# Row sums of a matrix-vector product moved from TensorE and VectorE to GpSimd, in the entry of a transformer trunk

## The chip, the cores and the metric

The kernel runs on one core of a Trainium2 chip. The core has five engines that work side by side, each through its own queue in order: TensorE (PE in the profile: matrix products, results in PSUM), VectorE (DVE), ScalarE (ACT), GpSimd (POOL) and SyncE (SP), which here issues DMAs. They wait for one another through semaphores. The metric is the device time of one execution in microseconds (us); of several runs the median counts.

## The reference

A trunk of two layers on 1024 rows of width 1024, all in float32. Each layer normalizes its input, modulates it by a shift and a scale that come from a conditioning vector `c`, and puts it through a mixer and an MLP. The part at issue is the first layer's modulation and the product behind it:

```python
c_act = jax.nn.silu(c)
mod = c_act @ ada_w[l] + ada_b[l]                  # 1024 x 6144
sh_m, sc_m, g_m, sh_f, sc_f, g_f = jnp.split(mod, 6, axis=-1)
h = modulate(rmsnorm(x, norm_g[l, 0]), sh_m, sc_m) # h * (1 + scale) + shift
bcx = h @ w_in                                     # 1024 x 3072
```

For the mixer's input the kernel needs only `sh_m` and `sc_m`, 2 x 1024 numbers, out of a product with 1024 x 2048 weights (8 MB). They are needed before the first product of the trunk can start.

## The kernel before, in words

The entry (`conv_phase`) makes the first column block of `h @ w_in` while the inputs come in. It works in eight blocks k = 0 to 7 of 128 columns of `h`. The weights of block k's shift and scale lie in a tile `aw[k]`: 128 partitions, 8 rows, 256 columns (128 of the scale, 128 of the shift). There are three such tiles in turn, so block k + 3 is loaded when block k has been read. What is wanted is the sum over 1024 inputs: over the 8 rows (each times its entry of the activated vector, `csil`) and over the 128 partitions. In the end it must stand in PSUM with one column per partition, summed over partitions by TensorE.

The table `rows_on_pe = (4, 4, 4, 4, 0, 0, 0, 0)` says how many of a block's eight rows TensorE takes by itself. For blocks 0 to 3 TensorE multiplies rows 0 to 3 straight from `aw` (`matvec`, 8 products, which the profile shows as 16 instructions), and VectorE sums rows 4 to 7 into a tile `av` (`row_sum`, one instruction a row). For blocks 4 to 7 VectorE sums all eight rows. Then TensorE adds `av` over the partitions with a matrix of ones (`row_end`).

The order of everything in the entry is written out by hand in the string `ENTRY`. Each word is one step, and each engine has its steps in just this order. The steps, with the line of the profile:

- `x`, `a`, `w`: loads of a row tile of x, of half of `aw[k]`, and of the mixer's weights of one block (SyncE, L196). They share one queue.
- `N`, `n`: the norm of a row tile (ScalarE L315 and L317, VectorE L322 and L1125).
- `A`: `matvec` (TensorE, L1018). `Dk.i`: `row_sum`, row i of block k (VectorE, L1025 the first and L1027 the others). `E`: `row_end` (TensorE, L1034). `F`: `shifts`, the scale and shift as columns (VectorE, L1039 and L1041).
- `T`: four transposes of x (TensorE, L1046). `U`, `W`: the modulated operand, rounded and plain (ScalarE, L1059). `L`: their difference (VectorE, L1064).
- `X`, `Y`: the mixer's weights split into two parts (ScalarE L1077, VectorE L1080).
- `M`: nine products of block k with one half of the rows (TensorE, L227). `Z`: products with zeros (TensorE, L1000).

Block k goes through a, A, D, E, F, then U, W, L, then M. A step that waits holds up everything behind it on its engine. GpSimd has no step in `ENTRY`; it fills four constants and `zeros` at the start and an accumulator in each of four later phases.

Of the kernel before, what the change touches and what calls it, by code (L numbers as in the profile page):

```python
# [8 lines left out]
F32 = mybir.dt.float32  # L9
# [3 lines left out]
ALU = mybir.AluOpType  # L13
# [4 lines left out]
P = 128  # L18
# [112 lines left out]
def trunk_kernel(ctx: ExitStack, tc: tile.TileContext, x, ada_w, ada_b, norm_g, conv_in_w, conv_out_w, kv_ada_w,  # L131
                 kv_a_w, kv_b_w, q_a_w, q_b_w, attn_o_w, mlp_up_w, mlp_down_w, columns, ada_first, conv_first,
                 consts, out):
    nc = tc.nc
    uid = [0]

    def nm(s):
        uid[0] += 1
        return f"{s}_{uid[0]}"

    def pool(name, side="left", **kw):
        return tc.alloc_tile_pool(name=name, bufs=1, side=side, reuse_waits="tile", **kw)
# [20 lines left out]
    def mm_ps():  # L163
        return ps.tile([P, HALF], F32, tag="mm", name=nm("mm"))

    def tp_ps():
        return ps.tile([P, HALF], F32, tag="tp", name=nm("tp"))
# [27 lines left out]
    def ld(out_, in_):  # L195
        nc.sync.dma_start(out_, in_)  # L196
# [5 lines left out]
    csil = cp.tile([P, KD], F32, name="csil")  # L202
# [767 lines left out]
    def conv_phase():  # L970
# [15 lines left out]
        st = pool("st", "right")  # L986
# [14 lines left out]

        aw, av, pa, tps, rts, raws, w = ({} for _ in range(7))
        acc = {}
        rows_on_pe = (4, 4, 4, 4, 0, 0, 0, 0)

        def load_x(t):
            ld(xt[t], x0[t * P:(t + 1) * P, :])
# [1 line left out]
        def load_ada(k, i):  # L1009
            if i == 0:  # L1010
                aw[k] = st.tile([P, KD, 2 * P], F32, tag="aw", name=nm("aw"), bufs=3)
            ld(aw[k][:, 4 * i:4 * i + 4, :], ada_first[k][:, 4 * i:4 * i + 4, :])

        def matvec(k):
            pa[k] = mm_ps() if k < 4 else tp_ps()
            for i in range(rows_on_pe[k]):
                for j in range(2):
                    nc.tensor.matmul(pa[k][:, j * P:(j + 1) * P], aw[k][:, i, j * P:(j + 1) * P],  # L1018
                                     csil[:, i:i + 1].to_broadcast([P, P]), start=i == j == 0, stop=False,
                                     skip_group_check=True)  # L1020

        def row_sum(k, i):
            if i == rows_on_pe[k]:
                av[k] = st.tile([P, 2 * P], F32, tag="av", name=nm("av"), bufs=2)
                nc.vector.tensor_scalar(av[k], aw[k][:, i, :], csil[:, i:i + 1], None, op0=ALU.mult)  # L1025
            else:
                nc.vector.scalar_tensor_tensor(av[k], aw[k][:, i, :], csil[:, i:i + 1], av[k], op0=ALU.mult, op1=ALU.add)  # L1027
# [96 lines left out]
        def norm_x(t):  # L1124
            nc.vector.tensor_scalar(xt[t], xt[t], rroot(rts[t]), None, op0=ALU.mult)  # L1125

        verbs = dict(Z=fill, x=load_x, a=load_ada, w=load_w, X=high_w, Y=low_w, N=root, n=norm_x, A=matvec, D=row_sum, E=row_end,
                     F=shifts, T=turn, U=lambda k, half: scaled(k, half, True), W=lambda k, half: scaled(k, half, False),
                     L=scaled_low, M=lambda k, half: products(k, half, acc))
# [68 lines left out]
    bg += ada_fm(ad, "s0f", w0, 4 * D, 32, gain(0, 2))  # L1198
    bg += ada_fm(ad, "h0f", w0, 3 * D, 24)
    conv_phase()  # L1200

    def down_phase(slots, sizes, wd, src_fn, g, xsrc, xdst, next_w, key, ys=None, pairs=True):
# [662 lines left out]
```

## Time and profile before

| | us |
|---|---|
| median of 3 runs | 2084.99 |
| lowest and highest run | 2084.24, 2086.21 |
| the profiled execution's time | 2085.6 |
| its span in the profile | 2083.8 |
| TensorE busy in the span | 2061.7 |
| VectorE busy | 1525.3 |
| ScalarE busy | 1058.7 |
| GpSimd busy | 4.6 |

The span runs from the first instruction to the last, and the execution's own time is 1.8 us longer. The matmuls are pipelined and their ends are modelled, so one that overlaps the next shows up as busy too. The entry is the first 68 us or so. In a row of the timeline the first two numbers are the start and the duration; x16 means that sixteen instructions of one kind are put into one row, and the bracket at the end says how long the engine stood idle before it and what it waited for.

### The profile page before, as it was taken

The numbers are of one execution on the slowest core, as the hardware profiler recorded it, in microseconds if no ns is written. First come the engines' busy times: TensorE is split into PE (matmuls) and PEld (weight loads), VectorE is DVE, ScalarE is ACT, GpSimd is POOL, SyncE is SP. The second block draws the span as 40 slices with busy tenths as digits, with TensorE's granted clock in tenths as the row PEclk, the third lists the DMA queues.
The fourth block names the chain that finished last, engine by engine and source line by source line (L and its number), as shares of the span: only waits on it lengthen the run. The fifth ranks groups of instructions, "written<-read, shape, count | busy, mean of one in ns | idle before, by whom it ended". The sixth has DMA issues, their size and how long they took to land.

```text
span 2083.8 us, 25410 instructions
## 1 busy us (share of the span) xinstructions
PE 2061.7 (99%) x9709; PEld 1716.1 (82%) x9709; DVE 1525.3 (73%) x2119; ACT 1058.7 (51%) x1506; POOL 4.6 (0%) x9
## 2 busy tenths in 40 slices
PE   8999999999999999999999999999999999999998
PEld 6888878888888888888888888878888888888887
DVE  7887776977665668876769999767976665559556
ACT  6533264845444533445756566556744454444342
POOL 0000000000000000000000000000000000000000
PEclk9999999999999999999999999999999999999999
DMA  7435464466443976556323232065455544753343
GB/s 284 116 120 151 142 219 136 120 200 210 152 156 119 325 236 229 163 198 199 98 73 87 76 109 88 31 202 162 113 184 173 187 160 178 268 193 111 101 142 142
DMA packets 222450, 330.86 MB, mean 159 GB/s; under 512 B 17268, under 2 KB 121972, under 8 KB 222328
## 3 DMA queue, kind: packets, MB, share of 16 engines
q1 hardware_dynamic: 184744, 248.68, 38.0%
q10 hardware_dynamic: 37584, 80.56, 10.3%
q8 instruction: 76, 1.25, 0.3%
q14 instruction: 46, 0.38, 0.1%
HBM read 248.45 MB, written 80.74 MB: 158 GB/s over the span
## 4 chain that ended last, share of the span: by engine, by line
PE 88%; DVE 7%; DMA 2%; ACT 2%; issue 1%; SPq 0%; DVEq 0%; ACTq 0%
PE one L227 41%; PE mm L227 20%; PE big L227 11%; PE tp L227 7%; PE big L1628 4%; PE tp L1660 1%; PE tp L1345 1%; DMA raw<-in_ada_w_dram 1%; ACT junk L315 1%; DVE y L366 1%; DMA w<-in_conv_first_dram 0%; DMA aw<-in_ada_first_dram 0%; DVE y L370 0%; PE tp L475 0%; DVE raw L345 0%
## 5 line engine op out<-in xcount | busy, mean ns | idle before, releaser
L227 PE MATMUL one<-slot,uphi 128*128 128x512 f32 x1240 | 381.7, 389 | 0.0
L227 PEld LDWEIGHTS one<-slot,uphi 128*128 128x128 f32 x1240 | 232.8, 188 | 48.4 <-issue 0.5
L227 PE MATMUL big<-slot 128*128 128x512 f32 x1152 | 264.1, 390 | 0.7 <-DVE y L1171 0.4
L227 PEld LDWEIGHTS big<-slot 128*128 128x128 f32 x1152 | 215.5, 188 | 45.7 <-ACT y L941 0.8
L227 PE MATMUL one<-slot,uplo 128*128 128x512 f32 x620 | 243.0, 392 | 2.4 <-DVE y L621 1.6
L230 ACT ACTIVATE ring<-w 128x1024 fp32r<-128x1024 f32 x98 | 103.8, 1059 | 260.5 <-PE tp L227 141.9
L227 PE MATMUL one<-ring,ring 128*128 128x512 f32 x1008 | 229.1, 389 | 0.0
L227 PEld LDWEIGHTS one<-ring,ring 128*128 128x128 f32 x1008 | 189.2, 188 | 39.3
L231 DVE TENSOR_TENSOR ring<-w,ring 128x1024 fp32r<-128x1024 f32 x98 | 119.8, 1223 | 116.8 <-ACT ring L230 116.7
L231 DVE TENSOR_TENSOR uplo<-raw,uphi 128x1024 fp32r<-128x1024 f32 x114 | 139.2, 1224 | 78.8 <-ACT uphi L230 78.8
L230 ACT ACTIVATE uphi<-raw 128x1024 fp32r<-128x1024 f32 x114 | 120.6, 1059 | 136.6 <-PE one L227 67.9
L227 PE MATMUL mm<-ring,ring 128*128 128x512 f32 x672 | 162.7, 390 | 1.2 <-DVE ring L231 1.2
L227 PE MATMUL tp<-ring,ring 128*128 128x512 f32 x672 | 161.6, 389 | 0.0
L227 PEld LDWEIGHTS mm<-ring,ring 128*128 128x128 f32 x672 | 125.5, 188 | 28.4 <-DVE ring L231 2.2
L227 PEld LDWEIGHTS tp<-ring,ring 128*128 128x128 f32 x672 | 126.1, 188 | 26.2
L227 PEld LDWEIGHTS one<-slot,uplo 128*128 128x128 f32 x620 | 116.4, 188 | 27.9 <-DVE y L621 2.4
L227 PE MATMUL mm<-slot,uphi 128*128 128x512 f32 x424 | 130.9, 390 | 0.0
L231 DVE TENSOR_TENSOR ring<-raw,ring 128x1024 fp32r<-128x1024 f32 x98 | 119.5, 1219 | 10.8 <-ACT ring L230 10.8
L227 PE MATMUL one<-slot,s 128*128 128x512 f32 x468 | 112.6, 389 | 1.6 <-DVE s L231 1.6
L256 DVE SCALAR_TENSOR_TENSOR acc<-raw,csil,acc 128x1024 f32<-128x1024 f32 x66 | 84.6, 1282 | 36.1 <-DMA raw<-in_ada_w_dram 35.0
L619 ACT ACTIVATE y<-one 128x512 f32<-128x512 f32 x62 | 36.7, 592 | 142.4 <-PE one L227 112.3
L230 ACT ACTIVATE ring<-raw 128x1024 fp32r<-128x1024 f32 x98 | 102.2, 1045 | 4.2 <-DMA raw<-ha 3.8
(291 smaller groups left out, 3509.3 us busy)
## 6 DMA issues: line engine op xcount, KB each, us to landing
ha<-y ACTq DMA_DIRECT2D x196, 256.0 KB, 3.0
raw<-ha SPq DMA_DIRECT2D x98, 512.0 KB, 4.2
raw<-in_ada_w_dram SPq DMA_DIRECT2D x80, 512.0 KB, 4.2
raw<-in_mlp_up_w_dram SPq DMA_DIRECT2D x70, 512.0 KB, 5.1
w<-in_mlp_down_w_dram SPq DMA_DIRECT2D x56, 512.0 KB, 5.1
raw<-hd SPq DMA_DIRECT2D x24, 512.0 KB, 4.5
xs<-raw ACTq DMA_DIRECT2D x24, 512.0 KB, 3.4
raw<-xs SPq DMA_DIRECT2D x24, 512.0 KB, 4.6
```

Of the source, the lines that this page charges most:

```text
L227: nc.tensor.matmul(out_, lhs[a], rhs[b], start=first and i == 0, stop=last and i == 2, skip_group_check=more)
L230: nc.scalar.activation(hi, src, AF.Copy)
L231: nc.vector.tensor_tensor(lo, src, hi.bitcast(F32), op=ALU.subtract)
L256: nc.vector.scalar_tensor_tensor(acc, raw, s, acc, op0=ALU.mult, op1=ALU.add)
L315: nc.scalar.activation(junk, src, AF.Square, accum_out=ss)
L366: nc.vector.tensor_tensor(y, y, p_, op=ALU.add)
L619: nc.scalar.activation(dst, x_, AF.Copy)
L1345: nc.tensor.transpose(p_[:, t * P:(t + 1) * P], ys[hf * 4 + t][:, k * P:(k + 1) * P], ident)
L1628: nc.tensor.matmul(o_, a, m_, start=j == 0, stop=j == 4)
L1660: nc.tensor.transpose(p_[:, c_:c_ + P], pts[h, 4 * hf + i][:, j * P:(j + 1) * P], ident)
```

## The change

`rows_on_pe` becomes (4, 0, 0, 0, 0, 0, 0, 0). In blocks 1 to 7 GpSimd takes rows 0 to 3: it multiplies them by their entries of `csil` in place (128x1024), adds rows 2 and 3 to rows 0 and 1 (128x512) and then row 1 to row 0 (128x256). VectorE takes rows 4 to 7; its first instruction adds GpSimd's row 0. Block 0 stays as it was.

```diff
-        rows_on_pe = (4, 4, 4, 4, 0, 0, 0, 0)
+        rows_on_pe = (4, 0, 0, 0, 0, 0, 0, 0)
+        pooled = 4
...
+        def pool_sum(k):
+            a = aw[k]
+            nc.gpsimd.tensor_tensor(a[:, :pooled, :], a[:, :pooled, :], csil[:, :pooled].unsqueeze(2).to_broadcast([P, pooled, 2 * P]),
+                                    op=ALU.mult)
+            nc.gpsimd.tensor_tensor(a[:, 0:2, :], a[:, 0:2, :], a[:, 2:4, :], op=ALU.add)
+            nc.gpsimd.tensor_tensor(a[:, 0, :], a[:, 0, :], a[:, 1, :], op=ALU.add)
+
         def matvec(k):
+            if not rows_on_pe[k]:
+                return pool_sum(k)
             pa[k] = mm_ps() if k < 4 else tp_ps()
...
         def row_sum(k, i):
-            if i == rows_on_pe[k]:
+            if not rows_on_pe[k] and i < pooled:
+                if i == 0:
+                    pool_sum(k)
+            elif not rows_on_pe[k] and i == pooled:
+                av[k] = st.tile([P, 2 * P], F32, tag="av", name=nm("av"), bufs=2)
+                nc.vector.scalar_tensor_tensor(av[k], aw[k][:, i, :], csil[:, i:i + 1], aw[k][:, 0, :], op0=ALU.mult, op1=ALU.add)
+            elif i == rows_on_pe[k]:
                 av[k] = st.tile([P, 2 * P], F32, tag="av", name=nm("av"), bufs=2)
                 nc.vector.tensor_scalar(av[k], aw[k][:, i, :], csil[:, i:i + 1], None, op0=ALU.mult)
```

`ENTRY` stays as it is: at the words A1, A2, A3 and at D4.0, D5.0, D6.0, D7.0 the three GpSimd instructions are issued, and the words Dk.1 to Dk.3 of blocks 4 to 7 do nothing. Lines behind the edit shift by 16: L1034 becomes L1050, L1046 L1062, L1064 L1080, L1080 L1096.

TensorE's queue from E0 on, before. The numbers behind the names tell the tiles apart; `tp_323` is filled from rows 0 to 511 of x.

```order
L1034 MATMUL mm_252<-ones,av_266 128x128 x2
L1018 MATMUL mm_295<-csil,aw_261 128x128 x8
L1000 LDWEIGHTS zeros
L1000 MATMUL one_187<-zeros 128x512
L1000 LDWEIGHTS zeros
L1000 MATMUL one_187<-zeros 128x512
L1046 MATMUL tp_323<-cs,y_165 128x128
L1046 MATMUL tp_323<-cs,y_166 128x128
L1046 MATMUL tp_323<-cs,y_167 128x128
L1046 MATMUL tp_323<-cs,y_168 128x128
L1034 MATMUL mm_295<-ones,av_308 128x128 x2
L1018 MATMUL mm_335<-csil,aw_304 128x128 x8
```

The same place with the change:

```order
L1050 MATMUL mm_252<-ones,av_266 128x128 x2
L1000 LDWEIGHTS zeros
L1000 MATMUL one_187<-zeros 128x512
L1000 LDWEIGHTS zeros
L1000 MATMUL one_187<-zeros 128x512
L1062 MATMUL tp_317<-cs,y_165 128x128
L1062 MATMUL tp_317<-cs,y_166 128x128
L1062 MATMUL tp_317<-cs,y_167 128x128
L1062 MATMUL tp_317<-cs,y_168 128x128
L1050 MATMUL mm_325<-ones,av_302 128x128 x2
L227 MATMUL one_344<-slot_151,w_194 128x512
L227 MATMUL one_344<-slot_151,w_193 128x512 x2
```

The rows of A1 and A2 (L1018) are gone, and behind E1 stands M0.0 (L227) at once.

VectorE's queue in block 4 (`av_468`) and the beginning of block 5 (`av_497`), before:

```order
L1025 TENSOR_SCALAR av_468<-aw_418,csil 128x256
L1027 SCALAR_TENSOR_TENSOR av_468<-aw_418,csil,av_468 128x256
L1064 TENSOR_TENSOR b_154<-raw_464,b_154 128x512
L1039 SCALAR_TENSOR_TENSOR sh_180<-mm_423,g_173,b_174 128x1
L1041 TENSOR_TENSOR sh_180<-mm_423,cols 128x1
L1027 SCALAR_TENSOR_TENSOR av_468<-aw_418,csil,av_468 128x256
L1025 TENSOR_SCALAR av_497<-aw_450,csil 128x256
L1027 SCALAR_TENSOR_TENSOR av_468<-aw_418,csil,av_468 128x256
L1027 SCALAR_TENSOR_TENSOR av_497<-aw_450,csil,av_497 128x256
L1027 SCALAR_TENSOR_TENSOR av_468<-aw_418,csil,av_468 128x256
L1064 TENSOR_TENSOR b_155<-raw_501,b_155 128x512
```

With the change block 4 is `av_488`:

```order
L1080 TENSOR_TENSOR b_154<-raw_448,b_154 128x512
L1055 SCALAR_TENSOR_TENSOR sh_180<-mm_455,g_173,b_174 128x1
L1057 TENSOR_TENSOR sh_180<-mm_455,cols 128x1
L1038 SCALAR_TENSOR_TENSOR av_488<-aw_408,csil 128x256
L1080 TENSOR_TENSOR b_155<-raw_485,b_155 128x512
L1043 SCALAR_TENSOR_TENSOR av_488<-aw_408,csil,av_488 128x256 x2
L1080 TENSOR_TENSOR slot_151<-q_161,slot_151 128x512
L1043 SCALAR_TENSOR_TENSOR av_488<-aw_408,csil,av_488 128x256
```

Four of block 4's eight row sums are gone, and the first one left (L1038) reads GpSimd's row of `aw` beside its own. The first rows that GpSimd's queue gains, blocks 1 and 2:

```order
L995 MEMSET zeros 128x512
L1017 ISA
L1017 TENSOR_TENSOR aw_261<-aw_261,csil 128x1024
L1019 TENSOR_TENSOR aw_261<-aw_261 128x512
L1020 TENSOR_TENSOR aw_261<-aw_261 128x256
L1017 TENSOR_TENSOR aw_298<-aw_298,csil 128x1024
L1019 TENSOR_TENSOR aw_298<-aw_298 128x512
```

Ahead of the first product stands one instruction that the order gives no operation for (ISA).

## The prediction

> **What bounds the kernel now.** I read the page first, for the share of each engine in the chain that ended last.
>
> ```profile
> span 2083.8 us, 25410 instructions
> ...
> PE 88%; DVE 7%; DMA 2%; ACT 2%; issue 1%; SPq 0%; DVEq 0%; ACTq 0%
> ```
>
> TensorE sets the end, and the change touches only the entry, so the question is how early TensorE gets its entry done. Next the busy times in stretches of 5 us over the entry:
>
> ```profile
> core 0: us, PE busy (x) PEld busy (x) DVE busy (x) ACT busy (x) POOL busy (x), PEclk, DMA share, GB/s
> 15.00:20.00 5.00, 5.00 (x36) 4.45 (x36) 3.37 (x10) 2.75 (x5) 0.00 (x0) 0.80 1.02 411
> 20.00:25.00 5.00, 5.00 (x36) 4.45 (x34) 4.50 (x12) 4.68 (x10) 0.00 (x0) 1.00 1.04 404
> 25.00:30.00 5.00, 5.00 (x37) 4.53 (x35) 4.53 (x13) 4.11 (x10) 0.00 (x0) 1.00 0.91 300
> 30.00:35.00 5.00, 5.00 (x29) 4.30 (x28) 3.81 (x12) 3.01 (x5) 0.00 (x0) 1.00 1.00 346
> 35.00:40.00 5.00, 4.38 (x26) 3.50 (x25) 5.00 (x12) 2.97 (x5) 0.00 (x0) 1.00 0.73 256
> 40.00:45.00 5.00, 5.00 (x26) 4.11 (x25) 4.62 (x13) 2.51 (x5) 0.00 (x0) 1.00 0.58 211
> 45.00:50.00 5.00, 4.79 (x28) 3.79 (x26) 3.83 (x11) 2.74 (x6) 0.00 (x0) 1.00 0.29 82
> 50.00:55.00 5.00, 5.00 (x29) 4.18 (x28) 4.67 (x13) 3.25 (x6) 0.00 (x0) 1.00 0.30 79
> ```
>
> From 15 us on TensorE is all but full (39.17 of 40 us), VectorE nearly so (34.33 of 40), the DMA engines are full up to 25 us and almost to 35, and GpSimd does nothing. Two engines are tight at once, and the change takes work from both. The timeline of TensorE, at the steps A (products of four rows, L1018), E (sum over partitions, L1034), M (L227) and at each later wait:
>
> ```profile
> 12.85 3.10 PE L1018 MATMUL mm<-csil,aw 128*128 128x128 f32 x16 [4.16 <-DMA aw<-in_ada_first_dram]
> ...
> 18.11 1.95 PE L1018 MATMUL mm<-csil,aw 128*128 128x128 f32 x16
> 19.90 0.59 PE L1000 MATMUL one<-zeros 128*128 128x512 bf16 x2
> ...
> 20.76 0.61 PE L1034 MATMUL mm<-ones,av 128*128 128x128 f32 x4
> 21.21 1.95 PE L1018 MATMUL mm<-csil,aw 128*128 128x128 f32 x16
> 22.92 2.32 PE L227 MATMUL one<-slot,w 128*128 128x512 f32 x9
> ...
> 25.51 0.61 PE L1034 MATMUL mm<-ones,av 128*128 128x128 f32 x4
> ...
> 28.05 1.95 PE L1018 MATMUL mm<-csil,aw 128*128 128x128 f32 x16
> 29.84 0.60 PE L1046 MATMUL tp<-cs,y 128*128 128x128 f32 x4
> ...
> 32.36 0.60 PE L1034 MATMUL mm<-ones,av 128*128 128x128 f32 x4
> ...
> 36.78 0.73 PE L227 MATMUL one<-b,w 128*128 128x512 f32 x2 [0.62 <-DVE b L1064]
> ...
> 49.55 0.63 PE L1046 MATMUL tp<-cs,y 128*128 128x128 f32 x4 [0.21 <-DVE sh L1041]
> ```
>
> The first row is A0; then A1, E1, A2, M0.0, E2, A3, T0.1, E3. After E3 TensorE waits only 0.62 and 0.21 us. VectorE in the same stretch (L1039 and L1041 are an F; L1025 and L1027 are row sums D; L1064 is an L):
>
> ```profile
> 18.31 0.22 DVE L1039 SCALAR_TENSOR_TENSOR sh<-mm,g,b 128x1 f32<-128x1 f32 x1 [0.58 <-PE mm L1034]
> 18.45 0.15 DVE L1041 TENSOR_TENSOR sh<-mm,cols 128x1 f32<-128x1 f32 x1
> 18.51 0.34 DVE L1025 TENSOR_SCALAR av<-aw,csil 128x256 f32<-128x256 f32 x1
> 18.89 1.52 DVE L1027 SCALAR_TENSOR_TENSOR av<-aw,csil,av 128x256 f32<-128x256 f32 x3
> 20.33 0.68 DVE L1064 TENSOR_TENSOR slot<-q,slot 128x512 fp32r<-128x512 f32 x1
> ...
> 22.47 0.35 DVE L1025 TENSOR_SCALAR av<-aw,csil 128x256 f32<-128x256 f32 x1
> ...
> 30.80 0.48 DVE L1027 SCALAR_TENSOR_TENSOR av<-aw,csil,av 128x256 f32<-128x256 f32 x1
> ...
> 53.68 1.00 DVE L1027 SCALAR_TENSOR_TENSOR av<-aw,csil,av 128x256 f32<-128x256 f32 x2
> ```
>
> Here D1 begins at 18.51, D2 at 22.47, D3.7 ends at 31.28 and D7.7 at 54.68.
>
> **TensorE's part.** A1, A2 and A3 go. From the start of each to the start of what follows it is 19.90 - 18.11 = 1.79, 22.92 - 21.21 = 1.71 and 29.84 - 28.05 = 1.79: 5.3 us of a full engine. But it does not reach the end. All three lie ahead of E3, E3 needs D3.7, and no VectorE instruction ahead of D3.7 is dropped: blocks 1 to 3 keep their four D each. D3.7 ended at 31.28 and E3 began at 32.36, so E3 can come at most 1.1 us earlier. Behind E3 TensorE's list is the same, with 0.83 us of waits. The gain is at most 1.1 + 0.8 = 1.9 us, however cheap GpSimd is; the other 3.4 us become waits for E1, E2 and E3.
>
> **VectorE's part.** It loses D4.0-D4.3 to D7.0-D7.3, and the first D of blocks 1 to 3 becomes a form with two tensor operands. Its groups in the first 70 us:
>
> ```profile
> L1027 DVE SCALAR_TENSOR_TENSOR av<-aw,csil,av 128x256 f32<-128x256 f32 x40 | 18.7, 482 | 0.5
> L1125 DVE TENSOR_SCALAR y<-y,small 128x1024 f32<-128x1024 f32 x8 | 6.0, 753 | 0.3
> L1064 DVE TENSOR_TENSOR slot<-q,slot 128x512 fp32r<-128x512 f32 x8 | 5.5, 687 | 1.2 <-ACT slot L1059 1.2
> L1025 DVE TENSOR_SCALAR av<-aw,csil 128x256 f32<-128x256 f32 x8 | 2.8, 350 | 1.6 <-DMA aw<-in_ada_first_dram 1.5
> L322 DVE RECIPROCAL small<-small 128x1 f32<-128x1 f32 x8 | 1.3, 161 | 4.5 <-ACT small L317 4.5
> ```
>
> 4 x (0.35 + 3 x 0.48) = 7.2 us go, 3 x (0.48 - 0.35) = 0.4 us come: 6.8 us less. This too pays only where TensorE waits for VectorE, the same 0.83 us.
>
> **GpSimd's part.** Seven blocks, each one product over 128x1024 and two sums over 128x512 and 128x256, each waiting for the one before. The trace has no GpSimd instruction that reads; nearest are its fills and the loads that release the first product:
>
> ```profile
> 0.73 0.52 POOL L995 MEMSET zeros<- 128x512 bf16 x1 [0.29 <-POOLq L1851]
> ...
> L246 POOL MEMSET acc<- 128x1024 f32 x3 | 2.9, 958 | 805.6 <-DVE uplo L704 726.8 <-DVE w L1080 78.8
> ...
> 5.61 1.57 SPq L196 DMA_DIRECT2D aw<-in_ada_first_dram  x2
> ...
> DMA to landing us min/median/max: 4.7/9.2/11.0
> ```
>
> One pass over 1024 elements is 0.96 us, over 512 0.52, so over 256 about 0.26. Lower bound: one pass each, 1.74 us a block. Upper bound: three passes (two operands in, one out), 5.2 us. I take two, since the fill already pays the writing and two operands must be fetched: 3.5 us, and 0.1 for the waits between: 3.6 us a block. The Trainium skill (GPSIMD Engine Reference, Performance versus the Vector engine) gives 4497 ns for a two-input add of 2048 elements; worked out from that, an estimate of 4.0 us a block, which would put the result below at +15 us instead of +12. No run here shows it yet.
>
> The first product needs the first half of block 1, issued at 5.61: at the longest landing time, 16.6 us. GpSimd alone then ends the blocks at 20.2, 23.8 and 27.4. D1.4 waits 20.2 - 18.5 = 1.7 us more than now, D2.4 1.3 us, D3.4 nothing. Queued behind D1.4 on VectorE are D1.5 to D1.7 and L0.0, for which E1 and M0.0 wait on TensorE. The shift of 1.3 to 1.7 us is partly paid out of A3, gone behind E2: about +1 us at E3, and from there to the end.
>
> **Sharing.** What decides is whether GpSimd and VectorE can read SBUF side by side. The trace cannot show it: GpSimd only writes there. Bounds: they do, +1 us; or only one of them runs at a time. I take the second. Its rows: one operand costs VectorE 753 ns for 1024 elements, 0.74 ns an element; two operands cost 687 for 512, 1.34 ns. One-operand instructions use a second path and two-operand ones need it, so nothing is spare for a third reader unless GpSimd has a path of its own. The Trainium skill (SBUF — State Buffer, Who interferes with whom) says that it has none: a VectorE instruction with two SBUF inputs, or in a two-port mode, and a GpSimd instruction that reads exclude each other for the whole instruction; no run here shows it yet, and by it the time is the one forecast here.
>
> The sum, from 16.6 us to the end of D7.7. VectorE's busy time there: about 2.5 of the first stretch (3.37 less D0's end before 16.6), then 4.50 + 4.53 + 3.81 + 5.00 + 4.62 + 3.83 + 4.67: 33.5. Less the 6.8 dropped: 26.7. Less what reads TensorE's results or single columns, seven F at 0.37 and three reciprocals at 0.16, 3.1: 23.6 us that exclude GpSimd. GpSimd: 7 x 3.6 = 25.2. One after the other: 16.6 + 23.6 + 25.2 = 65.4, against 54.7 now: +10.7. That is without a gap; VectorE stood idle 40 - 34.3 = 5.7 us in these stretches for others' results, and I let a quarter of it remain: +12. E7, F7, the last T, U, W, L and M hang on D7.7 in TensorE's and VectorE's queues and slip by the same. SP slips too: w3 waits for Y1 and a4 to a7 stand behind it; with the DMA engines idle from 45 us on (share 0.29) I add nothing. The profiled execution took 2085.6 us for its span of 2083.8, so 2085.6 + 12 = 2097.6; the median of the runs is 0.6 lower: **2097 us**.
>
> **Rivals.** 0.2% is 4.2 us, about what tells a change from none here.
> 1. No sharing: GpSimd reads without hindering VectorE. Then it is ready for D3 and all later blocks, and only D1 and D2 wait: +1 us, 2086 (from 2083 if GpSimd is at its lower bound, to 2089). For it: the block-1 wait is short and VectorE loses 6.8 us. It decides if VectorE's L1064 stays at 687 ns beside a running product.
> 2. GpSimd late or slower than I take it, without sharing: at 5.2 us a block it ends block 7 at 16.6 + 36.4 = 53 and D7.4-D7.7 (1.9 us) at 55, E2 some 4 to 5 us late: +5, 2090. The order shows an unnamed instruction ahead of its first product, without a price in the trace; the queue stands empty from 1.25 to 16.6, so 15 us of it are hidden and each one above comes on top of D1.4's wait. The Trainium skill (GPSIMD Engine Reference, Instruction dispatch) gives about 6 us for the first call of freshly loaded code: an estimate, and hidden here.
> 3. Faster by what TensorE loses, -5.3 us, 2080: needs GpSimd's sums by 18.5 and VectorE ahead of TensorE up to E3; 9.0 busy of 10 us between 20 and 30 speaks against it.
>
> **How the numbers follow.** Sharing 0.63, late or slow 0.14, no sharing 0.20, faster 0.03. In the likeliest case the lower bound of the price gives 16.6 + 23.6 + 7 x 1.9 = 53.5, no later than now but for D1 and D2, so +2; the upper 16.6 + 23.6 + 7 x 5.3 = 77.3: +23 and the gaps. TensorE's clock can add: A0, behind a wait of 4.16 us, took 3.10 us, into the stretch with a granted clock of 0.80, where A1 took 1.95. Ends near both bounds are unlikely together with sharing, so its own range is 2089 to 2107. No sharing lies around 2086, and the range that holds 8 in 10 takes most of it in: 2085.5 to 2107. Slower by over 0.2%: 0.63 x 0.96 + 0.14 x 0.8 + 0.20 x 0.1 + 0 = 0.74, to which I add a few hundredths for what only costs (clock, SP's queue): 0.78. Within: 0.19. Faster: 0.03.
>
> **What would show it.** Right: E1 at 22 to 25 instead of 20.76 with TensorE waiting for VectorE; L1038 rows released by GpSimd; L1064 and the other two-operand rows longer than 687 ns, or idle, beside a running product; E7 near 67 instead of 55.74; the same rows as now behind it. Wrong: two-operand rows at their old length beside GpSimd and E7 within 3 us of 55.74 (rival 1); GpSimd's product beginning after 17 us with its load long landed (rival 2); E3 before 31 (rival 3).

## The result, and the profile after

The changed kernel takes 2098.78 us (median of 6 runs, 2097.14 to 2101.01) against 2084.61 us before (median of 6, 2083.45 to 2086.21): the ratio is 1.0068, 95% interval 1.0055 to 1.0081. That is 14.2 us slower, where +12 was forecast.

The page of the changed kernel: the span, the busy times, and the chain by engine.

```profile
span 2096.0 us, 25328 instructions
...
PE 2063.1 (98%) x9660; PEld 1716.3 (82%) x9661; DVE 1536.1 (73%) x2103; ACT 1059.0 (51%) x1506; POOL 34.0 (2%) x30
...
PE 88%; DVE 7%; ACT 2%; DMA 2%; issue 1%; POOL 0%; SPq 0%; DVEq 0%; ACTq 0%; POOLq 0%
```

VectorE was given less to do and is busy for longer: 1536.1 us against 1525.3. Its groups in the first 80 us of the changed kernel say which rows grew (the last two columns ahead of the bar are the sum in us and the mean in ns):

```profile
L1043 DVE SCALAR_TENSOR_TENSOR av<-aw,csil,av 128x256 f32<-128x256 f32 x24 | 16.9, 702 | 0.5
L1038 DVE SCALAR_TENSOR_TENSOR av<-aw,csil 128x256 f32<-128x256 f32 x7 | 9.3, 1326 | 5.1 <-POOL aw L1020 5.1
L1141 DVE TENSOR_SCALAR y<-y,small 128x1024 f32<-128x1024 f32 x8 | 8.2, 1030 | 0.3
L1080 DVE TENSOR_TENSOR slot<-q,slot 128x512 fp32r<-128x512 f32 x8 | 6.6, 823 | 2.0 <-ACT slot L1075 2.0
```

In the kernel before, instructions of the same four forms had 482, 482, 753 and 687 ns. GpSimd's timeline beside VectorE's shows where the extra comes from. GpSimd, block 1 and the products of blocks 2 and 4:

```profile
16.65 1.89 POOL L1017 TENSOR_TENSOR aw<-aw,csil 128x1024 f32<-128x1024 f32 x1 [15.39 <-DMA aw<-in_ada_first_dram]
18.62 1.59 POOL L1019 TENSOR_TENSOR aw<-aw 128x512 f32<-128x512 f32 x1
20.29 0.72 POOL L1020 TENSOR_TENSOR aw<-aw 128x256 f32<-128x256 f32 x1
20.97 1.89 POOL L1017 TENSOR_TENSOR aw<-aw,csil 128x1024 f32<-128x1024 f32 x1
...
39.60 2.27 POOL L1017 TENSOR_TENSOR aw<-aw,csil 128x1024 f32<-128x1024 f32 x1 [8.38 <-DVE av L1043]
```

And VectorE's timeline of the same kernel:

```profile
16.95 2.14 DVE L1141 TENSOR_SCALAR y<-y,small 128x1024 f32<-128x1024 f32 x1
...
21.05 2.10 DVE L1038 SCALAR_TENSOR_TENSOR av<-aw,csil 128x256 f32<-128x256 f32 x1 [1.76 <-POOL aw L1020]
23.18 2.75 DVE L1043 SCALAR_TENSOR_TENSOR av<-aw,csil,av 128x256 f32<-128x256 f32 x3
25.84 0.68 DVE L1080 TENSOR_TENSOR slot<-q,slot 128x512 fp32r<-128x512 f32 x1
...
44.06 2.10 DVE L1038 SCALAR_TENSOR_TENSOR av<-aw,csil 128x256 f32<-128x256 f32 x1 [3.31 <-POOL aw L1020]
```

GpSimd's second product runs from 20.97 to 22.86. VectorE's D1.4 starts beside it at 21.05 and ends at 23.15: 0.3 us after the product, and 2.10 us instead of 0.48. L0.0 at 25.84, with no GpSimd instruction beside it, has its old length. It works the other way too: GpSimd's sum at 18.62 takes 1.59 us, while the shortest of its kind takes 1.28.

What TensorE waits for in the first 90 us of the changed kernel (us in total, how many times, the longest), with the rows of E1, M0.0, E2, E4 and E7 in its timeline:

```profile
PE mm L1050 <- DVE av L1043: 6.6, 2, 4.4
...
PE one L227 <- DVE b L1080: 4.3, 1, 4.3
PE tp L1062 <- ACT slot L1075: 2.3, 1, 2.3
...
PE tp L1050 <- ACT b L1075: 0.9, 1, 0.9
```

```profile
25.98 1.22 PE L1050 MATMUL mm<-ones,av 128*128 128x128 f32 x4 [4.44 <-DVE av L1043]
26.86 3.66 PE L227 MATMUL one<-slot,w 128*128 128x512 f32 x9
...
33.07 1.14 PE L1050 MATMUL mm<-ones,av 128*128 128x128 f32 x4 [2.12 <-DVE av L1043]
...
53.43 1.20 PE L1050 MATMUL tp<-ones,av 128*128 128x128 f32 x4 [0.91 <-ACT b L1075]
...
71.20 0.61 PE L1050 MATMUL tp<-ones,av 128*128 128x128 f32 x4
```

E1 is 5.2 us late (25.98 against 20.76), E2 7.6, E4 14.3 (53.43 against 39.16) and E7 15.5 (71.20 against 55.74). The loss is made in blocks 1 to 4, and behind E4 TensorE runs through. The new waits are 6.6 + 4.3 + 2.3 + 0.9 = 14.1 us. The old ones of 0.8 and TensorE's dropped 5.3 come off: 8.0. The other 7.5 us of the 15.5 stand in slower products: M0.0 takes 3.66 instead of 2.32, and the granted clock is 0.52 between 25 and 30 us, where the kernel before had 1.00. Whether those 7.5 us are a cause of their own is asked below.

The profiled executions lie 12.2 us apart at the end, not 15.5. About 2.6 us of this is seen in later waits: the kernel before had waits of 0.8 and 1.2 us that the changed one doesn't have, and one of 1.6 us that is now 1.0. In the kernel before:

```profile
PE one L227 <- DVE s L231: 1.6, 1, 1.6
...
PE mm L227 <- DVE ring L231: 1.2, 1, 1.2
...
PE one L227 <- ACT y L689: 0.8, 1, 0.8
```

These belong to one execution each; over all runs the difference is 14.2.

### The profile page after: what moved, and what is told of

It is laid out like the page before. It is cut to its first block, busy times and chain, and to the rows that moved or that the text cites. A ratio compares the mean times of both kernels' runs of the same rounds, so it can differ in the third digit from the quotient of the medians.

```text
span 2096.0 us, 25328 instructions
## 1 busy us (share of the span) xinstructions
PE 2063.1 (98%) x9660; PEld 1716.3 (82%) x9661; DVE 1536.1 (73%) x2103; ACT 1059.0 (51%) x1506; POOL 34.0 (2%) x30
## 4 chain that ended last, share of the span: by engine, by line
PE 88%; DVE 7%; ACT 2%; DMA 2%; issue 1%; POOL 0%; SPq 0%; DVEq 0%; ACTq 0%; POOLq 0%
PE one L227 41%; PE mm L227 20%; PE big L227 11%; PE tp L227 7%; PE big L1644 4%; PE tp L1676 1%; PE tp L1361 1%; ACT junk L315 1%; DMA raw<-in_ada_w_dram 1%; DMA aw<-in_ada_first_dram 1%; DVE y L366 1%; DVE y L370 0%; DVE raw L345 0%; PE tp L475 0%; PE one L240 0%
## 5 line engine op out<-in xcount | busy, mean ns | idle before, releaser
L227 PE MATMUL one<-slot,uphi 128*128 128x512 f32 x1240 | 382.0, 389 | 0.0
L227 PEld LDWEIGHTS one<-slot,uphi 128*128 128x128 f32 x1240 | 232.8, 188 | 48.5 <-issue 0.5
L227 PE MATMUL big<-slot 128*128 128x512 f32 x1152 | 264.1, 390 | 0.5 <-DVE y L1187 0.4
L227 PEld LDWEIGHTS big<-slot 128*128 128x128 f32 x1152 | 215.4, 188 | 45.6 <-ACT y L941 0.5
L227 PE MATMUL one<-slot,uplo 128*128 128x512 f32 x620 | 243.1, 392 | 1.6 <-DVE y L621 1.6
L227 PE MATMUL one<-ring,ring 128*128 128x512 f32 x1008 | 229.1, 389 | 0.0
L227 PEld LDWEIGHTS one<-ring,ring 128*128 128x128 f32 x1008 | 189.2, 188 | 39.3
L227 PE MATMUL mm<-ring,ring 128*128 128x512 f32 x672 | 162.4, 390 | 0.0
L227 PE MATMUL tp<-ring,ring 128*128 128x512 f32 x672 | 161.6, 389 | 0.0
L227 PEld LDWEIGHTS tp<-ring,ring 128*128 128x128 f32 x672 | 126.1, 188 | 26.2
L227 PEld LDWEIGHTS mm<-ring,ring 128*128 128x128 f32 x672 | 125.6, 188 | 26.8 <-DVE ring L231 0.5
L227 PEld LDWEIGHTS one<-slot,uplo 128*128 128x128 f32 x620 | 116.4, 188 | 27.1 <-DVE y L621 2.4
L227 PE MATMUL mm<-slot,uphi 128*128 128x512 f32 x424 | 131.0, 390 | 0.0
L227 PE MATMUL one<-slot,s 128*128 128x512 f32 x468 | 112.6, 389 | 1.0 <-DVE s L231 1.0
L256 DVE SCALAR_TENSOR_TENSOR acc<-raw,csil,acc 128x1024 f32<-128x1024 f32 x66 | 84.6, 1282 | 32.6 <-DMA raw<-in_ada_w_dram 31.3
```

The source lines that it names most:

```text
L227: nc.tensor.matmul(out_, lhs[a], rhs[b], start=first and i == 0, stop=last and i == 2, skip_group_check=more)
L256: nc.vector.scalar_tensor_tensor(acc, raw, s, acc, op0=ALU.mult, op1=ALU.add)
```

## The experiments

Two explanations stood against each other at first. *Exclusion*: VectorE and GpSimd keep each other from SBUF, and the sum of their work sets the time. *Lateness*: GpSimd's sums come too late, and the rest waits. Each experiment's time stands beside that of the kernel before on the same chip.

**GpSimd reads, and nobody waits for it.** The kernel before, with GpSimd's instructions added on the side.

```diff
+        spill = st.tile([P, 4, 2 * P], F32, name="spill")
+        def pool_sum(k):
+            a = aw[k]
+            nc.gpsimd.tensor_tensor(spill, a[:, :4, :], csil[:, :4].unsqueeze(2).to_broadcast([P, 4, 2 * P]), op=ALU.mult)
+            nc.gpsimd.tensor_tensor(spill[:, 0:2, :], spill[:, 0:2, :], spill[:, 2:4, :], op=ALU.add)
+            nc.gpsimd.tensor_tensor(spill[:, 0, :], spill[:, 0, :], spill[:, 1, :], op=ALU.add)
         def matvec(k):
+            if k > 0:
+                pool_sum(k)
...
         def row_sum(k, i):
+            if k >= 4 and i == 0:
+                pool_sum(k)
```

> The kernel before, in which GpSimd also makes the 21 instructions of blocks 1 to 7, into a scratch tile that nobody reads; TensorE and VectorE keep all their work, and only the reload of an aw tile waits for GpSimd. Exclusion theory: VectorE's two-operand rows beside a GpSimd instruction stretch (0.48 and 0.69 us to as much as 2.1), and the time rises by 8 to 20 us over the kernel before, to 2093-2105, though no result is waited for. Lateness theory (the loss is the wait for GpSimd's results, no exclusion): VectorE's rows keep 0.48 and 0.69, time 2084-2087.

2104.39 us against 2084.78: ratio 1.0098 (1.0083 to 1.0113), +19.6 us. VectorE's groups in the first 75 us:

```profile
L1039 DVE SCALAR_TENSOR_TENSOR av<-aw,csil,av 128x256 f32<-128x256 f32 x40 | 31.4, 798 | 0.5
L1137 DVE TENSOR_SCALAR y<-y,small 128x1024 f32<-128x1024 f32 x8 | 7.4, 926 | 0.3
...
L1076 DVE TENSOR_TENSOR b<-raw,b 128x512 fp32r<-128x512 f32 x4 | 4.9, 1214 | 0.0
```

482 ns have become 798 and 686 have become 1214 on an unchanged list. No result of GpSimd is used, so lateness cannot explain it. One wait for GpSimd is left, that for the reload of an `aw` tile, but none of the waits of SyncE's queue in the first 90 us ends with GpSimd. The run costs more than the change itself; VectorE and TensorE keep all their work here.

**GpSimd only writes.** The kernel before, with seven times three fills of about the same lengths, one behind the other from 1.2 to 32.1 us.

```diff
+        spill = st.tile([P, 2048], BF16, name="spill")
+        def pool_fill(k):
+            for n in (2048, 1408, 768):
+                nc.gpsimd.memset(spill[:, :n], float(k))
...
+        for k in range(7):
+            pool_fill(k)
```

> The kernel before, with 21 fills on GpSimd of about the same lengths (2048, 1408 and 768 bfloat16, 0.94 ns each: about 29 us from 1.3 us on), which read nothing. Exclusion of readers only: VectorE's two-operand rows keep 0.48 and 0.69, time within 1.5 us of the kernel before. Exclusion by any GpSimd instruction: rows up to 2 us long in the first 30 us, time 2090 or more. Lateness theory: as the kernel before.

2088.42 us against 2084.78: ratio 1.0020 (1.0011 to 1.0030), +3.6 us. That is between the two expectations, and the groups say why:

```profile
L1033 DVE SCALAR_TENSOR_TENSOR av<-aw,csil,av 128x256 f32<-128x256 f32 x40 | 18.6, 481 | 0.5
L1131 DVE TENSOR_SCALAR y<-y,small 128x1024 f32<-128x1024 f32 x8 | 10.3, 1282 | 0.3
...
L1031 DVE TENSOR_SCALAR av<-aw,csil 128x256 f32<-128x256 f32 x8 | 6.9, 865 | 1.1 <-DMA aw<-in_ada_first_dram 1.0
L1070 DVE TENSOR_TENSOR slot<-q,slot 128x512 fp32r<-128x512 f32 x8 | 5.5, 686 | 1.2 <-ACT slot L1065 1.2
```

The two-operand rows keep their 481 and 686 ns, as expected. The one-operand rows do not: 753 ns became 1282 and 350 became 865. I had not separated these two kinds for writes.

**The changed kernel with writes in place of reads.** GpSimd is waited for at the same places; rows 0 to 3 of blocks 1 to 7 are left out of the result.

```diff
-            nc.gpsimd.tensor_tensor(a[:, :pooled, :], a[:, :pooled, :], csil[:, :pooled].unsqueeze(2).to_broadcast([P, pooled, 2 * P]),
-                                    op=ALU.mult)
-            nc.gpsimd.tensor_tensor(a[:, 0:2, :], a[:, 0:2, :], a[:, 2:4, :], op=ALU.add)
-            nc.gpsimd.tensor_tensor(a[:, 0, :], a[:, 0, :], a[:, 1, :], op=ALU.add)
+            for n, times in ((4, 2), (2, 3), (1, 3)):
+                for _ in range(times):
+                    nc.gpsimd.memset(a[:, :n, :], 0.0)
```

> The changed kernel, in which GpSimd's 21 reading instructions are replaced by 56 fills of the same places (2 of 1024, 3 of 512 and 3 of 256 elements a block, about 4.3 us), which VectorE waits for as before; rows 0 to 3 of blocks 1 to 7 are thus left out of the result. Exclusion theory: no reader, so VectorE's rows keep their 0.48 and 0.69 us, and what is left is rival 1's price, +1 to +3: 2085-2088. Lateness theory: the waits for GpSimd are the same, so 2096-2101, as the changed kernel.

2091.42 us against 2084.78: ratio 1.0038 (1.0023 to 1.0053), +6.6 us. Neither number was met: half of the loss goes with the reads (7.6 us), half stays. The two-operand rows are back at 483 and 687 ns, the one-operand ones over 1024 elements are at 804. The fills last longer than what they replace (GpSimd is busy for 32.7 us with them, against 29.4), so GpSimd's own part in the lateness is not made smaller. What stays has two parts, seen in TensorE's timeline at E1 and at M1.1:

```profile
23.62 1.22 PE L1049 MATMUL mm<-ones,av 128*128 128x128 f32 x4 [3.24 <-DVE av L1042]
...
42.24 0.72 PE L227 MATMUL one<-b,w 128*128 128x512 f32 x2 [2.45 <-DVE b L1079]
```

The second hangs on block 4, whose loads stand behind w3 in SyncE's queue, and w3 waits for Y1 on a VectorE that is late. That gave the queue as a third suspect, and the clock was the fourth.

**Blocks 4 to 7 only, and blocks 1 to 3 only.** The table put back to (4, 4, 4, 4, 0, 0, 0, 0) in the first; in the second GpSimd's branch is left to blocks below 4.

```diff
-        rows_on_pe = (4, 0, 0, 0, 0, 0, 0, 0)
+        rows_on_pe = (4, 4, 4, 4, 0, 0, 0, 0)
```

```diff
-            if not rows_on_pe[k] and i < pooled:
+            if not rows_on_pe[k] and k < 4 and i < pooled:
...
-            elif not rows_on_pe[k] and i == pooled:
+            elif not rows_on_pe[k] and k < 4 and i == pooled:
```

> The changed kernel with GpSimd in blocks 4 to 7 only; TensorE keeps its rows of blocks 0 to 3. Exclusion theory: 4 x 4.0 = 16 us of GpSimd beside some 15 us of VectorE's two-operand work from about 31 us on put the end of D7.7 near 62 instead of 54.7: +4 to +8, 2089-2093. Lateness theory: each block's sums are there before VectorE comes to them, VectorE has 7.2 us less to do: -1 to +1, 2083.5-2085.5.

> The changed kernel with GpSimd in blocks 1 to 3 only; VectorE sums all eight rows of blocks 4 to 7 as before the change, TensorE keeps its rows of block 0 alone. The other half of the run with blocks 4 to 7 (+6.8 us). Exclusion theory: up to E3 everything is as in the changed kernel, E3 some 7.5 us late; behind it VectorE's rows have their old lengths again and nothing more is lost but what block 4's loads come late: +7 to +10, 2092-2095. If the loss came from TensorE's dropped rows being missed or from a single late block, it would be nearer to 0 or to the whole +14.

Blocks 4 to 7: 2091.55 us against 2084.78, ratio 1.0035 (1.0022 to 1.0048), +6.8. Blocks 1 to 3: 2091.63 against 2083.83, ratio 1.0037 (1.0026 to 1.0049), +7.8. Over the kernel before, both are where exclusion put them (+4 to +8, +7 to +10), and 6.8 + 7.8 = 14.6 is the whole loss. So the loss isn't made by a single late block, nor by TensorE's dropped rows: with TensorE's rows all kept and VectorE spared 7.2 us, blocks 4 to 7 still cost 6.8. How each half divides between exclusion and lateness, these two runs don't show. The expectation by lateness (-1 to +1) took every sum to be there in time; with blocks 4 to 7 alone VectorE still stands idle for 3.3 us until GpSimd's sums of block 4 are there, and D4.4, begun at 37.70 beside block 5's product, then takes 2.10 us.

**The clock.** The changed kernel with products that nobody reads in TensorE's waits (`R` repeats a transpose into its own tile). Only the changed words of `ENTRY`'s lines are shown.

```diff
-N6 Z2 T1.0 w1 L0.0 E1 w2
+N6 Z10 T1.0 w1 L0.0 Z12 E1 w2
...
-a3.1 E2 Y2 M1.0
+a3.1 Z6 E2 Y2 M1.0
...
-D4.5 M1.1
+D4.5 R2.1 R2.1 R2.1 R2.1 R2.1 R2.1 R2.1 R2.1 M1.1
...
-a7.0 L2.1 E4
+a7.0 L2.1 R3.1 R3.1 R3.1 R3.1 R3.1 E4
```

> The changed kernel with products that nobody reads in TensorE's waits: 8 more with zeros ahead of T1.0, 12 ahead of E1, 6 ahead of E2, and the transposes T2.1 and T3.1 made 8 and 5 times more ahead of M1.1 and E4. Clock theory (TensorE's granted clock falls to half behind each new wait, and its slower products are part of the loss): the clock stays at 1.00 from 25 us on and 2 to 4 us come back, 2095-2097. If only exclusion and lateness count: 2098-2100, as the changed kernel, since the slow products lie ahead of waits anyway.

2097.88 us against 2084.82: ratio 1.0067 (1.0052 to 1.0082), +13.1. The table by stretches of 10 us, at 20 to 30 and 50 to 60 us (the number behind the busy times is the granted clock):

```profile
20.00:30.00 10.00, 7.72 (x32) 5.23 (x33) 8.93 (x10) 4.90 (x10) 8.03 (x7) 0.83 0.64 251
...
50.00:60.00 10.00, 9.19 (x54) 7.76 (x53) 9.89 (x17) 3.31 (x5) 4.86 (x4) 1.00 0.44 147
```

In the changed kernel 50 to 55 us had 0.50, and 45 to 50 had 0.68. Here the clock is at 1.00 from 30 us on and the time is the same within the intervals: the slower products lay where TensorE would have waited. A wait is left at each of the five places (0.5 to 1.9 us), so the added products themselves cost nothing. M0.0 stays slow in this run (3.85 us, at a clock of 0.83 from 20 to 30 us); in the run with both edits, further down, it takes 2.31 us, and that run isn't faster. The intervals leave room for a gain of up to about 5 us, not for 7.5; nothing shows the clock to be a cause of its own.

**SyncE's queue.** Block 4's loads ahead of w3, in the changed kernel, then together with the fills of the clock run, then in the kernel with writes only (which leaves out the same rows as above). A part of the line is shown.

```diff
-E2 Y2 M1.0 N4 F2 w3 n7 w4 W2.0 a4.0 n4 A3 U2.0 D3.4 a4.1 D3.5
+E2 Y2 M1.0 N4 F2 a4.0 a4.1 w3 n7 w4 W2.0 n4 A3 U2.0 D3.4 D3.5
```

> The changed kernel with the two loads of block 4 ahead of w3 in SyncE's queue, so that they no longer wait for Y1. Queue theory: GpSimd's 8.4 us without work ahead of block 4 vanish, block 4's product begins near 31 instead of 39.6, and 3 to 7 us come back: 2092-2096. If the sum of VectorE's and GpSimd's work alone sets the end: the gap is filled, but the same two engines exclude each other there instead, and 0 to 2 us come back: 2097-2099.

> Both edits together, the fills in TensorE's waits and block 4's loads ahead of w3. If clock and queue are separate costs, their gains add up: 2088-2093. If exclusion takes them over, no better than the better of the two alone.

> The changed kernel with fills in place of GpSimd's reading instructions (rows 0 to 3 of blocks 1 to 7 left out of the result), and block 4's loads ahead of w3. What the late results cost without exclusion and without the queue: the fills alone were 6.6 us over the kernel before, and TensorE's wait of 2.4 us ahead of M1.1 stood behind block 4's loads; 2 to 4 us should come back: 2087-2090. If the queue has no part in it: 2091-2092.

With GpSimd reading: 2097.92 us against 2084.82, ratio 1.0067 (1.0052 to 1.0082), +13.1: no gain that can be told from none. Its timelines show where it went; GpSimd's block 4, then E2:

```profile
31.05 2.07 POOL L1017 TENSOR_TENSOR aw<-aw,csil 128x1024 f32<-128x1024 f32 x1
```

```profile
35.99 1.22 PE L1050 MATMUL mm<-ones,av 128*128 128x128 f32 x4 [4.84 <-DVE av L1043]
```

The gap ahead of block 4 is gone: its product starts at 31.05 instead of 39.60. E2 is at 35.99 instead of 33.07: the earlier product holds up VectorE's row sums of block 2, and GpSimd now stands for 7.2 us ahead of block 5. With the fills as well it is 2100.24 us, ratio 1.0077 (1.0060 to 1.0094), +15.4, no better than either alone. With writes only it is 2086.68 us, ratio 1.0012 (1.0003 to 1.0021): +1.9 in place of +6.6. So the queue counts where GpSimd only writes; where it reads, nothing of that can be seen.

## Why the prediction was right

**The mechanism** was the one forecast. With block 4's loads ahead of w3 in both kernels, the kernel that reads is at +13.1 us and the one that only writes at +1.9; the pair differs only in what GpSimd executes, and 11.2 us is the price of its reads there. In the queue as the change left it the same pair gives 14.2 - 6.6 = 7.6 us; the other 6.6 stay with writes only, and 4.7 of them go when block 4's loads are moved ahead. The rows beside GpSimd have about their length plus what is left of the GpSimd instruction, up to 2.15 us.

**TensorE's part.** That the gain is "at most 1.1 + 0.8 = 1.9 us, however cheap GpSimd is", fits: 5.3 us of dropped products went, and 14.1 us of waits came, 10.9 of them for VectorE and 3.2 for ScalarE. No run had GpSimd at no cost, so the bound itself wasn't tried.

**GpSimd's price.** 3.6 us a block were taken. The shortest rows of the changed kernel are 1.89, 1.28 and 0.72, 3.9 us. With what VectorE holds it up they are 1.97 + 1.40 + 0.85 = 4.2 us; from the start of the first product to that of the second (16.65 to 20.97) it is 4.3. The product came in at the estimate (1.92); the two sums were put too low, at 1.04 and 0.52. The estimate of 4.0 us worked out from the Trainium skill (GPSIMD Engine Reference, Performance versus the Vector engine) was nearer.

**The sum.** E7 was forecast near 67 and came at 71.2. Unhindered, a block takes 3.9 us and 0.2 between its rows, 4.1 instead of 3.6: by the forecast's own sum 7 x 0.5 = 3.5 us more. That is the term that was mis-sized. The path was another than the forecast had, too: it let E7 hang on the end of D7.7.

```profile
68.08 1.00 DVE L1043 SCALAR_TENSOR_TENSOR av<-aw,csil,av 128x256 f32<-128x256 f32 x2
```

D7.7 is the second of these two and ends at 69.08, 2.1 us ahead of E7. TensorE runs without a wait from E4 on, 14.3 us late there already, and ahead of D7.4 it is VectorE that waits for TensorE (0.78 us). So the loss is that of the waits up to E4, and GpSimd's last block, begun at 57.21, is not on the path. That the two engines' work, added up to a point for which TensorE didn't wait, came within 2.2 us of the measured change is in part luck; that they exclude each other is not.

"SP slips too ... I add nothing" was wrong as a reason (GpSimd stood for 8.4 us ahead of block 4). It did no visible harm to the sum: the run with that gap closed is no faster, though there a gap of 7.2 us stands ahead of block 5. The clock, kept as a possible extra, showed no price.

**Rival 1** was priced at +1 us. It measures +1.9 with block 4's loads ahead of w3 and +6.6 without: the step "then it is ready for D3 and all later blocks" left out those loads. With the queue as it is, a GpSimd that only writes still costs 6.6 us, more than the 0.2% (4.2 us) in which rival 1 stayed. The fills aren't quite its case, as they lengthen VectorE's one-operand rows.

**Rival 2.** Lateness alone is refuted by the run in which nobody waits for GpSimd (+19.6). The unnamed instruction ahead of the first product was hidden: the product starts at 16.65, released by its load. The Trainium skill's 6 us for freshly loaded code (GPSIMD Engine Reference, Instruction dispatch) are thus not shown by any run here: they may lie in the 15 us ahead of the product.

**Rival 3** needed E3 before 31; it came at 39.83.

## What to carry to other kernels

Work moved to an idle engine isn't free when that engine's reads hold up a busy one: here 29 us of GpSimd in the entry left VectorE busy for 10.8 us longer, although it was spared 6.8. Before moving work off a full engine, look whether the result can reach the end earlier at all; TensorE's 5.3 us could not by the argument of the prediction, which no run tried, since VectorE's list ahead of the same point was not shortened. To tell exclusion from lateness, let the second engine do the work into a scratch tile that nobody reads.

## What the runs showed of the hardware that was not expected

GpSimd's fills, which read nothing, slowed VectorE's one-operand instructions (753 to 1282 ns over 1024 elements, 350 to 865 over 256) and left the two-operand ones alone (481 and 686 ns); GpSimd's reads slowed both kinds. The Trainium skill (SBUF — State Buffer, Who interferes with whom) has both halves: two-operand instructions share only the read side with GpSimd, those in a two-port mode the pair. The rows agree, if the one-operand instructions run in such a mode, which no row here names. The Trainium skill's "fully blocks" in the same section agrees as well: 2.10 us for a 0.48 us instruction begun 0.08 us after a 1.89 us product.
